# Sample columns of the first FFN's gate and up: from the direct products of chunk 0 (256 of 320 columns stay) into the combined products of chunks 1 and 2 (416 columns each)

## The chip, the core and the metric

The kernel runs on one core of one Trainium2 chip. The metric is the device time of one launch in microseconds (us). Before the change the median of three runs is 1937.2 us (1936.32 to 1937.89).

A core has five engines with a queue each: TensorE (PE, matrix products into PSUM; loads of the stationary operand are shown as PEld), VectorE (DVE), ScalarE (ACT), GpSimd (POOL) and SyncE (SP), which here issues nearly all DMAs. SBUF has 128 partitions; "columns" are elements along the free dimension.

## What is computed

One layer of a decoder trunk, for a prompt of 1024 tokens and 64 sample tokens (8 sequences of 8), model width 1024, FFN width 2816:

```
x = x + 0.5 * post1(SwiGLU_1(pre1(x)))                  # first FFN
z = pre_mix(x) @ w_in + b_in                            # mixer: windowed attention and a gated recurrence
x = x + post_mix(concat(norm(attention), gate(recurrence)) @ w_out)
x = x + 0.5 * post2(SwiGLU_2(pre2(x)))                  # second FFN

def rms_norm(x, g):  return x * rsqrt(mean(x * x) + EPS) * g
def swiglu(x, w_gu, w_down):
    g, u = split(x @ w_gu, 2);  return (silu(g) * u) @ w_down
```

All of it is in float32. Outputs are the new x, the key and value windows and the recurrent states. The change concerns the first FFN above all: its pre-norm, its gate and up products, and its down product for one group of tokens.

## The kernel before

**Tokens.** The 1088 tokens lie in three chunks (`WIDTH = [320, 384, 384]`): chunk 0 has prompt tokens 0 to 255 and all 64 sample tokens, chunks 1 and 2 have 384 prompt tokens each. In the FFN's up part features lie on partitions and tokens along columns, in eight slices of 128 features.

**Precision.** Each float32 operand is split into a rounded part and a rest (`hi` by a ScalarE copy, L240; `lo` by a VectorE subtraction, L241), both in float32r. `mm3` (L258) makes a product of three matmuls, hi x hi, hi x lo, lo x hi, at L260, L261 and L262. So nearly every matmul of the trace has one of these three lines.

**Chunk 0 in the first FFN.** `up0` (L730) makes one tile of 128 gate and 128 up features: 2 x 8 x 3 = 48 matmuls of 320 columns. Weights are loaded and split by `load_w`, three weight tiles (of 24 matmuls) ahead (`loads0`, `Ahead`); the tag "wsp" has eight buffers, a hi and a lo for each of four weight tiles. The norm of chunk 0 isn't applied to its input: its root (`f.root`, one number a column) multiplies the gate and the up bank on their way out (`gated0`, L712: L718, L719, L725, L726). 18 of the 22 tiles are made so, ahead of the combined products (`HEAD1 = 9` pairs); the first three by hand in `pre_first`. The other four are cut into pieces (`piece`, L860) that stand between the combined products and use their weights; they need one more weight split, m = 8.

**Chunks 1 and 2 in an FFN.** Their gate and up products are combined: of the 2 x 2 blocks (two chunks, two halves of the features; gate, up) not eight but seven products are made (Strassen's scheme in Winograd's form). A "unit" is one tile of 128 gate and 128 up features for both chunks: 7 products x 4 slices x 3 = 84 matmuls of 384 columns; there are 22 units. The factors on the token side (`f.SF[1]` to `f.SF[7]`) are sums and differences of the normed chunks, made once by `pre_x` and `sums_s` (L525) in the stream `p1`. Those on the weight side are made for each unit by `factor` (L750; L760 and the splits), into buffers of the tags "wsp" and "wf" (4 buffers). `evict` (L790) takes the banks out and `left` (L821) sums them for the down part, which is again of seven products.

**Streams.** Side work is cut into steps by generators. `stream(name, gen, rate)` registers one, each `tick()` in the dense products makes `rate` steps of it, and `need(name)` makes all that are left. `p1` starts behind the first tile of the loop in the "f1" part and has 60 ticks there; `need("p1")` stands behind the head. In the same way `need("c2")` stands ahead of the second FFN's units.

**Order.** A planner of the framework places each engine's instructions from the program's order and its own estimate of times. An engine works in order; so does SP's queue of DMA issues.

**Down, chunk 0.** `down` (L942) makes 2 x 4 banks of 320 columns, and ScalarE copies each out (L963). Its token operand is read back from the DRAM tensor `acts` in pieces (`ar<-act`), through "wf" buffers.

**Mixer.** `mix_consts` (L147) makes masks at the end of the first FFN. The mixer's blocks of attention (`attn_block`, `finish_attn`) and recurrence run as streams beside the dense products of w_in, the rest of the first FFN's down part and the second FFN's head. Temporaries come from the tag "t2" (8 buffers), small columns from "small" (10).

Of the kernel before, what the change touches and what calls it, by code (L numbers as in the profile page):

```python
# [18 lines left out]
P = 128  # L19
# [6 lines left out]
WIDTH = [320, 384, 384]  # L26
BLK0 = [0, 2, 5]
# [20 lines left out]
def tile_step(ctx: ExitStack, tc: tile.TileContext, A: dict, O: list):  # L48
# [74 lines left out]
    ones = cp.tile([P, P], F32, name="ones")  # L123
    V.memset(ones, 1.0)
    junk = cp.tile([P, 512], BF16, name="junk")
    omean = cp.tile([P, P], F32, name="omean")
    V.memset(omean, 1.0 / D)
    S.activation(junk[:, :P], ones, AF.Silu)
    cols = cp.tile([P, NROWS], F32, name="cols")
    f1pre = cp.tile([P, KC], F32, name="f1pre")  # L130
    halfpost = cp.tile([P, 16], F32, name="halfpost")
    nsinkb = cp.tile([P, 8], F32, name="nsinkb")
    amask = cp.tile([P, 192], F32, name="amask")
    amask1 = cp.tile([P, P], F32, name="amask1")
    smask = cp.tile([P, 136], F32, name="smask")
    ssink = cp.tile([P, 2], F32, name="ssink")
    seqm = cp.tile([P, 4], F32, name="seqm")
    lmask = {h: cp.tile([P, 32], U8, name=f"lm{h}") for h in LEVELS[2:]}
    ident32 = cp.tile([P, 32], F32, name="ident32")
# [3 lines left out]
    def gains():  # L143
        nc.sync.dma_start(cols, A["cols"])
        V.tensor_scalar(halfpost[:, 0:8], cols[:, C_F1POST:C_F1POST + 8], 0.5, None, op0=ALU.mult)
        V.tensor_scalar(halfpost[:, 8:16], cols[:, C_F2POST:C_F2POST + 8], 0.5, None, op0=ALU.mult)

    def mix_consts():
# [4 lines left out]
        band = tmp2("band", (P, 256))  # L153
        V.memset(band, 0.0)
        G.affine_select(band, band, pattern=[[1, 256]], compare_op=ALU.is_ge, fill=NEG,
                        base=0, channel_multiplier=-1)
        G.affine_select(band, band, pattern=[[-1, 256]], compare_op=ALU.is_ge, fill=NEG,
                        base=P, channel_multiplier=1)
        V.tensor_copy(amask[0:64], band[0:64, 0:192])
        V.tensor_copy(amask[64:P], band[64:P, 64:256])  # L160
        V.tensor_copy(amask1, amask[:, 64:192])
        V.memset(amask1[0:64, 0:64], NEG)
# [5 lines left out]

        s5 = tmp[:, 3, 0:32]
        V.tensor_scalar(s5, row[:, 0:32], 31, None, op0=ALU.bitwise_and)  # L170
        V.tensor_tensor(x[:, 0:32], col[:, 0:32], s5, op=ALU.bitwise_xor)
        V.tensor_copy(tf[:, 1, 0:32], s5)
        V.tensor_copy(tf[:, 1, 32:64], col[:, 0:32])
        V.tensor_tensor(tf[:, 0, 0:32], tf[:, 1, 32:64], tf[:, 1, 0:32], op=ALU.is_gt)
        V.tensor_tensor(ident32, tf[:, 1, 32:64], tf[:, 1, 0:32], op=ALU.is_equal)
        for i, h in enumerate(LEVELS[2:]):
            V.tensor_scalar(tmp[:, 3, 32:64], x[:, 0:32], 4 - i, None, op0=ALU.logical_shift_right)
            V.tensor_copy(tf[:, 1, 64:96], tmp[:, 3, 32:64])
            V.scalar_tensor_tensor(lmask[h], tf[:, 1, 64:96], 1.0, tf[:, 0, 0:32],
                                   op0=ALU.is_equal, op1=ALU.mult)  # L180
# [16 lines left out]
        V.tensor_tensor(smask, tf2[:, 2], tf2[:, 3], op=ALU.add)  # L197

        e = cp.tile([P, 3, 4], F32, name="lbe")
# [34 lines left out]
    def small():  # L234
        return pp.tile([P, 4, 8], F32, tag="small", bufs=10, name=uid("sm"))
# [51 lines left out]
    def tmp2(name, shape=(P, 512)):  # L287
        return pp.tile(list(shape), F32, tag="t2", bufs=8, name=uid(name))
# [177 lines left out]
    def factor(SF, m, src):  # L466
        new = (lambda: hslot(1)) if m in (1, 2, 4, 5) else (lambda: big(F32R))
        hi, lo = SF[m] = new(), new()
        S.copy(hi, src)
        yield  # L470
        V.tensor_tensor(lo, src, hi.bitcast(F32), op=ALU.subtract)
        yield

    def pre_x(n, y, gpre, part, SF):
# [5 lines left out]
        yield from bcast_steps(x_part, 384, rb, True)  # L480
# [10 lines left out]
    def pre_s(n, y, gpre, part, SF, dst=None):  # L491
# [15 lines left out]
        for kh in range(2):  # L507
            a = big()
            part[n].append(a)
            for k in range(4):  # L510
# [4 lines left out]
                if k % 2:  # L515
                    V.tensor_scalar(a[:, k], bank[:, :384], g, None, op0=ALU.mult)
                else:
                    S.activation(a[:, k], bank[:, :384], AF.Copy, scale=g)
# [6 lines left out]
    def sums_s(part, SF):  # L525
        (a11, a12), (a21, a22) = part[1], part[2]
        s1, s2 = big(), big()
# [13 lines left out]
    x2T = dr.tile([P, KC, WIDTH[0]], F32, name="x2T")  # L541
    x1N = [dr.tile([384, D], F32, name=f"x1N{n}") for n in range(2)]
    x2N = [dr.tile([384, D], F32, name=f"x2N{n}") for n in range(2)]

    def load_x(n):
        y = [big(), big()]
        for hf in range(2):
            nc.sync.dma_start(y[hf], A["xT"][n - 1][:, 4 * hf * 384:4 * (hf + 1) * 384].rearrange("p (k t) -> p k t", k=4))
# [5 lines left out]
    def load_first(ws):  # L554


        w = WIDTH[0]
        x = [big(F32, (P, 4, w)), big(F32, (P, 4, w))]
        raws = [big(F32, (P, KC, P)) for _ in ws]

        def x_cols(d, n):
            nc.sync.dma_start(x[d // 4][:, d % 4:d % 4 + n], x0_part(d, n))
# [19 lines left out]
    def pre_first(x, gpre, h, raws, wts):  # L582
# [3 lines left out]
        w = WIDTH[0]  # L586
        spare = axbank()
        for _ in range(WARM):
            warm = PE.matmul(spare[:, :P], ones, ones, start=True, stop=True).ins
# [78 lines left out]
        order("V", made[2])  # L668
# [1246 lines left out]
```

## Time and profile before

| | |
|---|---|
| median of three runs | 1937.2 us (1936.32 to 1937.89) |
| span of the profiled execution | 1937.4 us |
| HBM read / written | 290.86 / 83.39 MB |
| mean DMA rate over the span | 193 GB/s |
| first FFN: head and units | 0 to about 494 us |
| down, chunk 0 | about 494 to 571 us |
| mixer and what runs beside it | about 640 to 1330 us |
| second FFN's units and down | from about 1386 us |

The stages are read from TensorE's instructions in order of time. The profile was taken by the hardware's profiler in one execution. Busy time of an engine is the time covered by its instructions. A matmul's record lasts longer than the distance to the next one's start, since they are pipelined, so a busy TensorE says nothing yet of its pace; the distance from start to start does.

### The profile page before, as it was taken

To read this page: it belongs to the slowest core of one execution; us is meant where nothing else is said; L and a number is where in the kernel's file an instruction comes from. 1 tells how busy PE (TensorE), PEld (TensorE's weight loads), DVE (VectorE), ACT (ScalarE), POOL (GpSimd) and SP (SyncE) were. 2 spreads that over 40 slices of the span, in tenths; PEclk is the share of its full clock that TensorE was granted. 3 is DMA by queue.
4 is the path that set the end of the run, shared out by engine and by line. 5 is a ranking of instruction groups with operands and counts; after the bars stand their busy time and mean duration, and the time that the engine had idled before them with its cause. 6 is when DMAs were issued, how large, how long until landed. Compare 5 with 4: busy or idle time off the path is not lost.

```text
span 1937.4 us, 34843 instructions
## 1 busy us (share of the span) xinstructions
PE 1923.1 (99%) x13547; PEld 1806.1 (93%) x13547; DVE 1430.7 (74%) x2469; ACT 946.0 (49%) x1701; POOL 186.1 (10%) x227
## 2 busy tenths in 40 slices
PE   9999999999999999999999999999999999999998
PEld 9999999999998987788999888989999999999886
DVE  6896789877568666787678758756987887656666
ACT  5553444444455434545445545846544444445452
POOL 0300000000004022020221212000000000000102
PEclk9999999999999999999999999999999999999999
DMA  6643676555767556765334344546555555667974
GB/s 248 209 133 115 232 267 247 206 191 184 242 217 242 180 155 215 283 220 163 114 102 153 99 140 142 164 147 209 185 198 192 198 188 189 210 228 241 308 255 141
DMA packets 175750, 375.56 MB, mean 194 GB/s; under 512 B 16144, under 2 KB 67536, under 8 KB 175568
## 3 DMA queue, kind: packets, MB, share of 16 engines
q1 hardware_dynamic: 169680, 362.84, 56.0%
q10 hardware_dynamic: 5904, 10.49, 1.5%
q8 instruction: 106, 1.74, 0.4%
q14 instruction: 60, 0.49, 0.1%
HBM read 290.86 MB, written 83.39 MB: 193 GB/s over the span
## 4 chain that ended last, share of the span: by engine, by line
PE 88%; DMA 6%; DVE 3%; ACT 1%; issue 1%; POOL 1%; SPq 0%; ACTq 0%; DVEq 0%; POOLq 0%
PE mm L260 27%; PE mm L262 26%; PE mm L261 26%; DMA ar<-fa 1%; DMA xt<-in_x_rest_dram 1%; DMA ar<-act 1%; PE lv L1337 1%; PE sc L1237 1%; DMA raw<-in_ffn_w_gu_dram 1%; PE pv L1283 1%; DVE w L241 1%; PE pT L1269 1%; PE c L262 0%; PE c L260 0%; PE c L261 0%
## 5 line engine op out<-in xcount | busy, mean ns | idle before, releaser
L260 PE MATMUL mm<-h,wsph 128*128 128x320 f32 (+1 forms) x1344 | 427.2, 319 | 0.4 <-DVE big L814 0.4
L261 PE MATMUL mm<-h,wsph 128*128 128x320 f32 (+1 forms) x1344 | 425.5, 317 | 0.2 <-DVE h L241 0.2
L262 PE MATMUL mm<-h,wspl 128*128 128x320 f32 (+1 forms) x1344 | 422.6, 316 | 0.0
L241 DVE TENSOR_TENSOR wspl<-raw,wsph 128x1024 fp32r<-128x1024 f32 x208 | 260.8, 1255 | 125.2 <-ACT wsph L240 124.1
L240 ACT CAST wsph<-raw 128x1024 fp32r<-128x1024 f32 x208 | 217.8, 1049 | 254.0 <-PE mm L261 199.3
L260 PEld LDWEIGHTS mm<-h,wsph 128*128 128x128 f32 x1344 | 252.2, 188 | 4.2 <-issue 2.3
L261 PEld LDWEIGHTS mm<-h,wsph 128*128 128x128 f32 x1344 | 252.5, 188 | 3.9 <-issue 2.3
L262 PEld LDWEIGHTS mm<-h,wspl 128*128 128x128 f32 x1344 | 251.9, 188 | 3.4 <-issue 3.1
L240 ACT CAST w<-raw 128x512 fp32r<-128x512 f32 (+1 forms) x208 | 153.8, 745 | 199.9 <-PE mm L261 96.2
L261 PE MATMUL mm<-h,w 128*128 128x384 f32 (+1 forms) x736 | 245.6, 334 | 0.3 <-DVE h L622 0.3
L260 PE MATMUL mm<-h,w 128*128 128x384 f32 (+1 forms) x736 | 245.7, 334 | 0.2 <-ACT h L620 0.2
L262 PE MATMUL mm<-h,w 128*128 128x384 f32 (+1 forms) x736 | 239.6, 333 | 0.5 <-POOL w L613 0.4
L241 DVE TENSOR_TENSOR w<-raw,w 128x512 fp32r<-128x512 f32 (+1 forms) x208 | 178.3, 861 | 72.6 <-ACT w L240 71.7
L261 PE MATMUL mm<-w,h 128*128 128x512 f32 x462 | 180.5, 391 | 0.7 <-DVE w L241 0.7
L260 PE MATMUL mm<-w,h 128*128 128x512 f32 x462 | 180.8, 394 | 0.0
L262 PE MATMUL mm<-w,h 128*128 128x512 f32 x462 | 179.8, 391 | 0.0
L260 PE MATMUL mm<-big,w 128*128 128x384 f32 x528 | 176.7, 335 | 0.3 <-ACT big L806 0.2
L261 PE MATMUL mm<-big,w 128*128 128x384 f32 x528 | 176.5, 334 | 0.0
L262 PE MATMUL mm<-big,w 128*128 128x384 f32 x528 | 176.0, 334 | 0.0
L261 PEld LDWEIGHTS mm<-h,w 128*128 128x128 f32 x736 | 138.1, 188 | 1.1 <-DVE h L622 0.8
L260 PEld LDWEIGHTS mm<-h,w 128*128 128x128 f32 x736 | 138.1, 188 | 0.8 <-ACT h L620 0.5
L262 PEld LDWEIGHTS mm<-h,w 128*128 128x128 f32 x736 | 137.6, 188 | 1.0 <-POOL w L613 0.7
(367 smaller groups left out, 3353.8 us busy)
## 6 DMA issues: line engine op xcount, KB each, us to landing
raw<-in_ffn_w_gu_dram SPq DMA_DIRECT2D x162, 512.0 KB
raw<-in_ffn_w_down_dram SPq DMA_DIRECT2D x74, 512.0 KB
raw<-in_w_in_dram SPq DMA_DIRECT2D x54, 512.0 KB
ar<-fa SPq DMA_DIRECT2D x70, 384.0 KB
big<-in_ffn_w_down_dram SPq DMA_DIRECT2D x88, 256.0 KB
fb<-big SPq DMA_DIRECT2D x44, 512.0 KB
fa<-big SPq DMA_DIRECT2D x22, 768.0 KB
raw<-fb SPq DMA_DIRECT2D x30, 512.0 KB
```

The source lines that it names most:

```text
L240: made['S'] = S.copy(hi, src).ins
L241: (lo_eng or V).tensor_tensor(lo, src, hi.bitcast(F32), op=ALU.subtract)
L260: PE.matmul(out, a[0], b[0], start=first, stop=False, skip_group_check=resume)
L261: PE.matmul(out, a[0], b[1], start=False, stop=False, skip_group_check=resume)
L262: return PE.matmul(out, a[1], b[0], start=False, stop=last, skip_group_check=resume).ins
L1237: PE.matmul(banks[g][rows(hq), i, cs], zq[rows(g), 2 * pr + i, b * P + 64 * hq:b * P + 64 * hq + 64], kx[rows(g), k0 + cs.start:k0 + cs.st ...
L1269: PE.transpose(tb2[hq][:, g, i, slot], pt[g][rows(hq), c:c + P], ident[rows(hq), rows(hq)])
L1283: PE.matmul(ob[par][rows(g), :, hq], vn[rows(par), b + (blk + hq) // 2, rows(g)], pT[hq][rows(par), g, :, PLACE[hq][blk]], start=alone or ...
L1337: PE.matmul(b5[32 * i:32 * i + 32, b, a], K[:, a, cs], Q[:, a, cs], start=True, stop=True)
```

## The change

Each of the chunks 1 and 2 takes 32 sample tokens into the first FFN's gate and up part, as columns 384 to 415 behind its own (`WS = 416`); chunk 0 keeps 256 prompt columns there (`WU`). The host lays the input out so. All 22 tiles of chunk 0 are now made in the head (`HEAD1 = NK`), and pieces, their step kinds and the split m = 8 are gone. `acts` gets prompt columns from `gated0` and sample columns from `evict`. Chunk 0's root is still applied to the gate, but for the up factor only at the down projection, on the 256 prompt columns, from a copy kept in DRAM (`rootd`). The sample columns are normed with their chunk.

The streams p1 and c2 are no longer emptied ahead of the units: a product takes the next steps of the stream until its factor is there (`feed`). p1 starts one tile earlier, chunk 1's input is loaded before the loop, and the split of factor 5 goes to GpSimd.

The wider buffers take room in SBUF. For it "t2" has 7 buffers, "small" 5 and "wf" 3; masks are made when the mixer starts (`amask` in bf16), or kept in DRAM (`smask`, `ownd`), the bias row is loaded for each chunk, and the attention's gain is applied behind the transposes, from the columns of `cols`. `f1pre` and the halved gains lie in `cols` too. In the second FFN's head ScalarE's Silu reads the bank directly.

```diff
+WU, XT = 256, 32
+WS = 384 + XT
...
-        return pp.tile([P, 4, w], F32R, tag=f"h{w}", bufs=8 if w == 384 else 4, name=uid("h"))
+        return pp.tile([P, 4, WS if w == 384 else w], F32R, tag=f"h{w}", bufs=8 if w == 384 else 4, name=uid("h"))
-    def big(dt=F32, shape=(P, 4, 384)):
+    def big(dt=F32, shape=(P, 4, WS)):
...
+    def feed(name):
+        gen = streams[name][0]
+        while True:
+            yield next(gen)
...
     def small():
-        return pp.tile([P, 4, 8], F32, tag="small", bufs=10, name=uid("sm"))
+        return pp.tile([P, 4, 8], F32, tag="small", bufs=5, name=uid("sm"))
-        return pp.tile(list(shape), F32, tag="t2", bufs=8, name=uid(name))
+        return pp.tile(list(shape), dt, tag="t2", bufs=7, name=uid(name))
...
     def factor(SF, m, src):
-        hi, lo = SF[m] = new(), new()
+        hi, lo = new(), new()
         S.copy(hi, src)
         yield
-        V.tensor_tensor(lo, src, hi.bitcast(F32), op=ALU.subtract)
+        (G if m in (5,) else V).tensor_tensor(lo, src, hi.bitcast(F32), op=ALU.subtract)
+        SF[m] = hi, lo
         yield
     def pre_x(n, y, gpre, part, SF):
-        yield from bcast_steps(x_part, 384, rb, True)
+        yield from bcast_steps(x_part, WS, rb, True)
...
         def gated0(j, g, rb):
-            w = WIDTH[0]
+            w = wu
             t = tmp2("sg")
-            if rb is None:
-                S.copy(t[:, :w], g[:, :w])
-            else:
+            if rb is not None:
                 V.tensor_tensor(t[:, :w], g[:, :w], rb, op=ALU.mult)
-            S.activation(t[:, :w], t[:, :w], AF.Silu)
+            S.activation(t[:, :w], g[:, :w] if rb is None else t[:, :w], AF.Silu)
             def rest(u):
-                v = u
-                if rb is not None:
-                    v = tmp2("su")
-                    V.tensor_tensor(v[:, :w], u[:, :w], rb, op=ALU.mult)
-                V.tensor_tensor(t[:, :w], t[:, :w], v[:, :w], op=ALU.mult)
-                return nc.sync.dma_start(acts[:, j], t[:, :w]).ins
+                V.tensor_tensor(t[:, :w], t[:, :w], u[:, :w], op=ALU.mult)
+                return nc.sync.dma_start(acts[:, j, :w], t[:, :w]).ins
...
-                w = f.pool.tile([P, 2, 512], F32R, tag="wf", bufs=4, name=uid("w"))
+                w = f.pool.tile([P, 2, 512], F32R, tag="wf", bufs=3, name=uid("w"))
...
         def product(u, m):
+            while m not in f.SF:
+                next(f.feed)
-            bk = chains[u, c][:, :384]
+            bk = chains[u, c][:, :ws]
...
         def evict(u, m):
             elif m == 3:
-                V.tensor_tensor(e[:, 1], bk, e[:, 1], op=ALU.add)
+                V.tensor_tensor(e[:, 1, :ws], bk, e[:, 1, :ws], op=ALU.add)
                 act(0)
+                if tag == 1:
+                    nc.sync.dma_start(acts[:, j, WU:].rearrange("p (h t) -> p h t", h=2), e[:, 0:3:2, 384:])
...
         def down(last=None):
+                    if tag == 1 and kp == NK - 2:
+                        rt = tmp2("rt")[:, :WU]
+                        nc.sync.dma_start(rt, rootd)
...
-                            S.copy(y[hf][:, i, :w], bank[:, :w])
+                            if tag == 1:
+                                V.tensor_tensor(y[hf][:, i, :WU], bank[:, :WU], rt, op=ALU.mult)
+                                S.copy(y[hf][:, i, WU:w], bank[:, WU:w])
+                            else:
+                                S.copy(y[hf][:, i, :w], bank[:, :w])
...
         def finish_attn(n, o, r, sl):
-            V.scalar_tensor_tensor(o[:r], o[:r], sm[:r, 1, 0:1], aon[:r], op0=ALU.mult, op1=ALU.mult)
+            S.activation(o[:r], o[:r], AF.Copy, scale=sm[:r, 1, 0:1])
...
-            put_mix(n, 0, sl, b4[:, :, :r])
+            hi, lo = MT[n][0][0], MT[n][1][0]
+            for c in range(4):
+                g = cols[:, C_AON + c:C_AON + c + 1]
+                S.activation(hi[:, c, sl], b4[:, c, :r], AF.Copy, scale=g)
+                V.scalar_tensor_tensor(lo[:, c, sl], b4[:, c, :r], g, hi[:, c, sl].bitcast(F32), op0=ALU.mult,
+                                       op1=ALU.subtract)
...
-    HEAD1, HEAD2 = 9, (4, 13, 22)
+    HEAD1, HEAD2 = NK, (4, 13, 22)
...
+        def p1():
+            yield from pre_x(1, xs[1], f1pre, part, f1.SF)
+            yield from pre_x(2, xs[2], f1pre, part, f1.SF)
+        xs.append(load_x(1))
         for j in first[3:]:
+            if j == first[3]:
+                stream("p1", p1(), P1)
             stored = f1.up0(j, w0)
-            if j in XAT:
+            if j == first[3]:
                 with tc.issue_after(stored):
-                    xs.append(load_x(len(xs)))
-            if j == XAT[0]:
-                def p1():
-                    yield from pre_x(1, xs[1], f1pre, part, f1.SF)
-                    yield from pre_x(2, xs[2], f1pre, part, f1.SF)
-                stream("p1", p1(), P1)
-        f1.begin(units(HEAD1))
-        need("p1")
+                    xs.append(load_x(2))
+        f1.begin(UNITS)
+        f1.feed = feed("p1")
...
-        f2.begin(units(NK))
-        need("c2")
+        f2.begin(UNITS)
+        f2.feed = feed("c2")
```

More of the change, by code (lines that the diff above doesn't have):

```diff
@@ L526, in sums_s @@
         (a11, a12), (a21, a22) = part[1], part[2]
-        s1, s2 = big(), big()
+        s1, s2 = [big()[:, :, :a11.shape[2]] for _ in range(2)]
         V.tensor_tensor(s1, a21, a22, op=ALU.add)
@@ L582, in pre_first @@
     def pre_first(x, gpre, h, raws, wts):
[L586 removed]
+        w = WU
         spare = axbank()
         for _ in range(WARM):
[L589 removed]
+            warm = PE.matmul(spare[:, :P], omean, omean, start=True, stop=True).ins
         tiles = [None] * len(raws)
```

256 lines of the change are left out of this document (125 added, 131 removed).

## The prediction, made before the changed kernel was built or run

> **What bounds the kernel now.** I read the page first, then the groups of instructions with shapes kept apart, then TensorE's timeline for the pace of one matmul, and last the windows for places where another engine is close behind.
>
> ```profile
> span 1937.4 us, 34843 instructions
> PE 1923.1 (99%) x13547; PEld 1806.1 (93%) x13547; DVE 1430.7 (74%) x2469; ACT 946.0 (49%) x1701; POOL 186.1 (10%) x227
> PE 88%; DMA 6%; DVE 3%; ACT 1%; issue 1%; POOL 1%; SPq 0%; ACTq 0%; DVEq 0%; POOLq 0%
> ```
> ```profile
> 60.00 0.31 PE L260 MATMUL mm<-h,wsph 128*128 128x320 f32 x1
> 67.04 0.31 PE L260 MATMUL mm<-h,wsph 128*128 128x320 f32 x1
> 380.16 0.33 PE L260 MATMUL mm<-big,w 128*128 128x384 f32 x1
> 384.32 0.33 PE L260 MATMUL mm<-h,w 128*128 128x384 f32 x1
> 622.70 0.39 PE L260 MATMUL mm<-w,h 128*128 128x512 f32 x1
> 624.74 0.39 PE L260 MATMUL mm<-w,h 128*128 128x512 f32 x1
> ```
>
> TensorE is busy 99% of the span, and the chain that ended last is 88% TensorE. What a matmul costs is not its duration (0.31 us), because they overlap, but the distance from start to start. The three pairs of rows are the ends of 48, 24 and 9 intervals (48 is sixteen rounds of L260, L261, L262): 7.04/48 = 146.7 ns at 320 columns, 4.16/24 = 173.3 ns at 384, 2.04/9 = 226.7 ns at 512. The three lie on one line: 13.3 ns plus 0.4167 ns a column. By it 256 columns take 120.0 ns and 416 take 186.7 ns (estimates; neither width runs in this trace).
>
> The profile gives a span and no other time of its own execution. 1937.4 us lies 0.2 above the median of the three runs, so differences worked out from it are taken off 1937.2.
>
> **The columns.** The direct products of chunk 0 are 22 tiles x 2 (gate, up) x 8 slices x 3 = 1056 matmuls: 18 tiles in the head (864) and 4 as pieces between the combined products (192).
>
> ```profile
> L260 PE MATMUL mm<-h,w 128*128 128x384 f32 x704 | 235.4, 334 | 0.0
> ...
> L260 PE MATMUL mm<-big,w 128*128 128x384 f32 x528 | 176.7, 335 | 0.3 <-ACT big L806 0.2
> ```
>
> The two groups of one of three lines give (704 + 528) x 3 / 2 = 1848 combined products for each FFN. All counts stay. The direct products go from 146.7 to 120.0 ns: 1056 x 26.7 ns = 28.2 us less. The combined ones go from 173.3 to 186.7 ns: 1848 x 13.3 ns = 24.6 us more. Net **-3.5 us** (before rounding). The fixed part cancels; what is left is 1056 x 64 - 1848 x 32 = 8448 columns.
>
> The unknown is the pace at 256. The nearest rows on both sides are 320 columns, 146.7 ns, and transposes of 128 columns, each with a weight load of its own.
>
> ```profile
> 828.23 1.47 PE L457 MATMUL tr<-ident,big 128*128 128x128 f32 x12
> ```
> ```profile
> L457 PE MATMUL tr<-ident,big 128*128 128x128 f32 x48 | 7.1, 273 | 0.0
> ```
>
> Twelve of them take 1.47 us, the last 0.27 of it its own duration, so (1.47 - 0.27)/11 = 109 ns. Loads of 128 columns can follow each other at least that fast, so they don't stop a pace of 120.0 ns, which I take. The ends are 109 ns (11.6 us more gained) and 146.7 ns (28.2 us not gained); from 123.3 ns on the change costs matmul time instead of saving it.
>
> **VectorE while chunks 1 and 2 are prepared.** The stream p1 (norm, gains, sums and their splits) runs beside the direct tiles, whose own VectorE work is two weight splits and three (after: two) products with a bank.
>
> ```profile
> 100.00:132.00 32.00, 32.00 (x220) 32.00 (x219) 32.00 (x39) 16.94 (x18) 0.00 (x0) 1.00 0.46 136
> 60.00:100.00 40.00, 40.00 (x273) 39.73 (x272) 34.87 (x46) 22.14 (x30) 8.98 (x6) 1.00 0.58 187
> ```
> ```profile
> L241 DVE TENSOR_TENSOR wspl<-raw,wsph 128x1024 fp32r<-128x1024 f32 x8 | 9.7, 1218 | 0.0
> L483 DVE SCALAR_TENSOR_TENSOR big<-big,f1pre,rb 128x384 f32<-128x384 f32 x8 | 4.4, 608 | 0.0
> L471 DVE TENSOR_TENSOR big<-big,big 128x1536 fp32r<-128x1536 f32 x2 | 3.5, 1750 | 0.0
> L471 DVE TENSOR_TENSOR h<-big,h 128x1536 fp32r<-128x1536 f32 x2 | 3.5, 1750 | 0.0
> L725 DVE TENSOR_TENSOR su<-mm,rb 128x320 f32<-128x320 f32 x5 | 2.4, 485 | 0.0
> L718 DVE TENSOR_TENSOR sg<-mm,rb 128x320 f32<-128x320 f32 x5 | 2.4, 484 | 0.0
> L726 DVE TENSOR_TENSOR sg<-sg,su 128x320 f32<-128x320 f32 x4 | 1.9, 485 | 0.0
> L530 DVE TENSOR_TENSOR big<-big,big 128x1536 f32<-128x1536 f32 x1 | 1.8, 1751 | 0.0
> ```
> ```profile
> L241 DVE TENSOR_TENSOR wspl<-raw,wsph 128x1024 fp32r<-128x1024 f32 x11 | 15.0, 1367 | 2.2 <-ACT wsph L240 2.2
> L726 DVE TENSOR_TENSOR sg<-sg,su 128x320 f32<-128x320 f32 x5 | 4.3, 861 | 0.1
> ...
> L725 DVE TENSOR_TENSOR su<-mm,rb 128x320 f32<-128x320 f32 x6 | 2.9, 481 | 0.0
> L718 DVE TENSOR_TENSOR sg<-mm,rb 128x320 f32<-128x320 f32 x5 | 2.4, 483 | 0.1
> ```
>
> In a row of the windows stand the stretch, its length, then busy time and count of PE, PEld, DVE, ACT and POOL, the clock granted (1.00) and the DMA share and rate. From 100 to 132 us VectorE is busy for all of 32.00 us, and TensorE still runs dense (220 matmuls x 146.7 ns = 32.3 us). It is the one place where another engine is at its limit. The eight groups are those of 100 to 132 us, the four behind them of 60 to 100.
>
> From 100 to 132 there are 220/48 = 4.6 tiles. The groups add up to 35.5 us (four like L530, and one of 0.6 us) in 32.00, because successive instructions overlap: a factor of 0.90. p1 has 19.1 of them, 17.2 us by the factor; the tiles 14.8. After, p1 is 416/384 as wide and one of its splits (1.75 us) goes to GpSimd: 17.2 x 1.083 - 1.7 = 16.9 us. A tile needs 2 x 1.218 us for the splits and two products of 256 columns at 0.41 us (an estimate from 0.484 us at 320, 0.0011 us a column), so 4.6 x 3.26 x 0.90 = 13.5 us. Together that is 30.4 us in 4.6 x 48 x 120.0 ns = 26.5 us of matmuls: **3.9 us too much.** From 60 to 100 us (5.7 tiles) the tiles have 24.6 x 0.90 = 22.1 us of the 34.87, p1 12.8; after, 12.8 x 1.083 + 5.7 x (2 x 1.367 + 0.82) x 0.90 = 32.1 of 32.8 us, so nothing is saved up there.
>
> GpSimd's split has a price too.
>
> ```profile
> 50.85 1.65 DVE L241 TENSOR_TENSOR wspl<-raw,wsph 128x1024 fp32r<-128x1024 f32 x1
> 53.64 2.04 DVE L241 TENSOR_TENSOR wspl<-raw,wsph 128x1024 fp32r<-128x1024 f32 x1
> 56.01 1.64 DVE L241 TENSOR_TENSOR wspl<-raw,wsph 128x1024 fp32r<-128x1024 f32 x1
> 50.25 6.31 POOL L311 TENSOR_TENSOR ss<-ss,sq 128x384 f32<-128x384 f32 x4
> ```
> ```profile
> L1585 POOL TENSOR_TENSOR big<-big,big 128x1024 f32<-128x1024 f32 x4 | 10.0, 2511 | 32.0 <-PE sav L1582 32.0
> ```
>
> Beside 6.31 us of GpSimd additions three VectorE splits took 1.65, 2.04 and 1.64 us instead of 1.218: 1.7 us too much, 0.27 us for each us of GpSimd. A split of 1664 columns is about 2.51 x 1664/1024 = 4.1 us on GpSimd, so it adds 1.1 us: 5.0 us too much in all.
>
> The Trainium skill, "SBUF — State Buffer", section "Who interferes with whom", says that a VectorE instruction with two SBUF inputs and a GpSimd one that reads SBUF shut each other out for the whole instruction. By that rule the 4.1 us would be lost whole, and the wait below 3.0 us longer. The row of 2.04 us shows only a part of the time lost, and the measurement decides.
>
> ```profile
> L240 ACT CAST wsph<-raw 128x1024 fp32r<-128x1024 f32 x208 | 217.8, 1049 | 254.0 <-PE mm L261 199.3 <-DMA raw<-in_ffn_w_down_dram 16.5 <-issue 11.8
> ```
>
> The cover is that weights are split three tiles of 24 matmuls ahead: 3 x 24 x 120.0 ns = 8.6 us, less one cast and one split (1.05 + 1.22), so 6.3 us if it is full when the stretch begins. 5.0 fits in 6.3, but little refills it before. I take **+1.0 us** of waiting TensorE. The ends are 0 and 9.6 us: no cover, and no overlap of instructions, so that full durations count in both stretches (33.8 - 26.5 = 7.3; 20.2 + 13.8 - 32.8 = 1.2; the lock 1.1).
>
> **The other edits.**
>
> ```profile
> 0.00:20.00 20.00, 17.80 (x104) 16.35 (x105) 13.09 (x25) 15.51 (x29) 1.98 (x7) 1.00 0.84 305
> 470.00:500.00 30.00, 29.38 (x181) 28.86 (x180) 20.18 (x59) 17.68 (x27) 0.33 (x2) 1.00 0.58 195
> 715.00:900.00 185.00, 182.39 (x1621) 150.18 (x1620) 141.55 (x314) 87.72 (x198) 36.39 (x39) 1.00 0.68 226
> 1130.00:1330.00 200.00, 199.27 (x2035) 178.61 (x2034) 134.88 (x286) 119.42 (x254) 20.50 (x32) 1.00 0.48 154
> ```
> ```profile
> 481.29 3.67 DMA ar<-act
> ```
>
> Four more tiles bring eight weight loads of 512 KB into the head: 1 MB for each 5.76 us, 182 GB/s, where the first 20 us moved 305. Chunk 1's input goes ahead of the tiles on SP's queue, before the fourth raw weight: 1.7 MB at 305 GB/s is 5.6 us, covered by the weights already loaded. In the units a VectorE operation grows by 32 x 0.0011 us and the unit by 84 x 13.3 ns = 1.1 us, so there is more cover than before. Forming products lazily instead of emptying p1 and c2 first, and masks that no longer fall at the end of the first FFN, can remove the 0.62 us of idle TensorE from 470 to 500 us; I take **-0.3**.
>
> At the down projection the eviction is a product on VectorE beside a small copy, under six matmuls of the next bank: nothing. There "wf" has three buffers for four, and the last unit's sample columns are stored just before they are loaded. If a load comes late, the next weights wait behind it on SP, and it costs one landing like the 3.67 us row. Two tiles of 24 x 146.7 ns = 7.0 us hide it; I take 0, end +3.7.
>
> In the mixer the norm's gain moves behind the transposes, six instructions more for each of nine blocks; ScalarE has 178 of 385 us idle in the two windows of it. Fewer "t2" (7 for 8) and "small" (5 for 10) buffers can make blocks wait for one another. TensorE idles 2.6 + 0.7 us there now; I take **+0.3**, from -2 to twice that idle time again, +4.
>
> Sum: -3.5 + 1.0 - 0.3 + 0.3 = -2.5, so **1934.7 us**.
>
> **The rivals.** (1) *All of it is kept*: the splits stay ahead and idle places go, -3.5 - 0.6 - 1.3 (of the mixer's -2) = **1931.8 us**. For it: the cover of 6.3 us. (2) *VectorE becomes the bound in p1*, the slower end: TensorE waits for weight splits. The full 9.6 us give 1937.2 - 3.5 + 9.6 = **1943.3 us**; from 7.4 us of waiting on, the result is slower than before by 0.2%. For it speaks 32.00 of 32.00; against it, that TensorE stayed dense beside that. (3) *The weight load sets the pace at 256*: at 146.7 ns nothing is saved there, -3.5 + 28.2, **1961.9 us**; against it stands the 109 ns. The Trainium skill, "TensorE: Matmul & The Clock Gate", section "LDWEIGHTS (loading the stationary operand)", gives a load its columns divided by 1.2 in ns, an estimate from that page of 106.7 ns for 128; 256 columns stream just as long, so a load would have no room left, yet the 109 ns agrees with the page and lies under 120. (4) *Fewer buffers in the mixer*, at their end: -3.5 + 1.0 - 0.3 + 4 = **1938.4 us**, and 1942.1 with the late load at the down projection. (5) *The change doesn't bring what it says*: columns are saved, and waits take all of it, **1937.2 us**.
>
> **How the numbers follow.** A measurement of this kernel can tell about 0.2%, 3.9 us. Forecast 0.40, its own range 1933.4 to 1937; (1) 0.36; (2) 0.11; (3) 0.03; (4) 0.06, half of it with the late load; (5) 0.04. Faster by over 0.2%: 0.36. Within: 0.40 + 0.03 + 0.04 = 0.47. Slower: 0.11 + 0.03 + 0.03 = 0.17. The range takes in (1), (4), (5) and the nearer part of (2): 1929.5 to 1942.5.
>
> **What would show it.** Right: 120.0 ns from start to start at 256 columns and 186.7 at 416; VectorE full for some 26 us of the head, with TensorE's weight loads waiting there about 1 us for splits; a smaller VectorE share in the units. Wrong: a pace above 123 ns; several us of weight loads waiting for VectorE in the head; a longer stretch between the two FFNs.

## The result and the profile after

| | before | after |
|---|---|---|
| median | 1937.55 us (1936.32 to 1939.19, 4 runs) | 1970.56 us (1967.74 to 1972.76, 4 runs) |
| ratio | | 1.0166, 95% interval 1.0152 to 1.0180 |
| span of the profiled execution | 1937.4 us | 1966.0 us |

The change makes the kernel 33 us slower; forecast was 1934.7 us with an upper end of 1942.5. The profiled execution of after is the fastest of its four, so the traces have to account for the 28.6 us between the two spans. Of the page of after, the span, the busy time of the engines, and the chain that ended last:

```profile
span 1966.0 us, 35068 instructions
...
PE 1942.7 (99%) x13547; PEld 1810.9 (92%) x13547; DVE 1441.1 (73%) x2474; ACT 960.3 (49%) x1719; POOL 203.4 (10%) x230
...
PE 85%; DVE 5%; DMA 4%; ACT 2%; issue 2%; POOL 1%; SPq 0%; ACTq 0%; DVEq 0%; POOLq 0%
```

The same 13547 matmuls, TensorE still "busy" for 99%, and yet 19.6 us more of it (1942.7 against 1923.1). The share says nothing of it, and it is a first hint that the matmuls themselves have become slower. The starts of the first matmul of each stage in TensorE's timeline give the lengths of the stages (us):

| stage | before | after | difference |
|---|---|---|---|
| first FFN: head and units | 485.8 | 496.2 | +10.4 |
| first FFN: down, chunk 0 | 73.9 | 73.2 | -0.7 |
| first down pair to the second FFN's units (mixer) | 808.7 | 819.6 | +10.9 |
| second FFN: units | 325.2 | 327.9 | +2.7 |
| second FFN: down, chunk 0, and the down pairs | 230.6 | 235.8 | +5.2 |

The second FFN's units and pairs have the same instructions and shapes as before. TensorE's timeline of after tells what happened there. The rows are pairs: the first and the last of 48 intervals at 256 columns, 84 at 416, 84 at 384 (second FFN), 30 at 512 (second FFN's pairs).

```profile
121.81 0.28 PE L245 MATMUL mm<-h,wsph 128*128 128x256 f32 x1
127.58 0.28 PE L245 MATMUL mm<-h,wsph 128*128 128x256 f32 x1
379.75 0.35 PE L244 MATMUL mm<-big,w 128*128 128x416 f32 x1
395.62 0.35 PE L244 MATMUL mm<-big,w 128*128 128x416 f32 x1
1499.75 0.34 PE L246 MATMUL mm<-h,w 128*128 128x384 f32 x1
1514.49 0.34 PE L246 MATMUL mm<-h,w 128*128 128x384 f32 x1
1879.67 0.40 PE L245 MATMUL mm<-w,h 128*128 128x512 f32 x1
1886.67 0.40 PE L245 MATMUL mm<-w,h 128*128 128x512 f32 x1
```

5.77/48 = 120.2 ns at 256 columns, as forecast. 15.87/84 = 188.9 ns at 416, not 186.7. 14.74/84 = 175.5 ns at 384, where it was 173.3, and 7.00/30 = 233.3 ns at 512, where it was 226.7. TensorE waits for no other engine in these stretches: the matmuls themselves are a little slower.

The head is another matter. The windows of after (columns as in the prediction) and its waits from 60 to 120 us:

```profile
60.00:80.00 20.00, 16.47 (x132) 15.74 (x131) 18.78 (x21) 11.75 (x19) 12.26 (x6) 1.00 0.62 196
100.00:120.00 20.00, 16.85 (x124) 16.30 (x123) 20.00 (x18) 10.80 (x11) 5.05 (x1) 0.91 0.35 118
```
```profile
PE rb L279 <- POOL ss L295: 2.6, 1, 2.6
PE mm L244 <- DVE sg L705: 2.6, 2, 1.4
...
PEld mm L244 <- ACT big L453: 1.5, 1, 1.5
...
PE mm L244 <- DVE sg L709: 0.9, 1, 0.9
...
PE mm L246 <- DVE wspl L225: 0.6, 1, 0.6
```

132 and 124 matmuls need about 15.8 and 14.9 us at 120.0 ns, so 4.2 and 5.1 us are lost, **9.3 us** in all. The listed waits of TensorE's matmuls are 6.7 us of it. One, 2.6 us, is its own matmul of the root (`rb`, L279), which waits for GpSimd's additions. The others end on VectorE: 3.5 us on the products that read a gate or an up bank (L705, L709) and so set it free, and only 0.6 us on a weight split (L225). One weight load (PEld) waits 1.5 us for ScalarE. In the second stretch the granted clock also falls to 0.91; its listed waits are 3.2 us, and 5.1 are lost.

### The profile page after: what moved, and what is told of

The parts are those of the page before. It is cut to its first block, busy times and chain, and to the rows that moved or that the text cites. A ratio compares the mean times of both kernels' runs of the same rounds, so it can differ in the third digit from the quotient of the medians.

```text
span 1966.0 us, 35068 instructions
## 1 busy us (share of the span) xinstructions
PE 1942.7 (99%) x13547; PEld 1810.9 (92%) x13547; DVE 1441.1 (73%) x2474; ACT 960.3 (49%) x1719; POOL 203.4 (10%) x230
## 4 chain that ended last, share of the span: by engine, by line
PE 85%; DVE 5%; DMA 4%; ACT 2%; issue 2%; POOL 1%; SPq 0%; ACTq 0%; DVEq 0%; POOLq 0%
PE mm L244 27%; PE mm L245 27%; PE mm L246 27%; DMA raw<-in_ffn_w_gu_dram 1%; DVE wspl L225 1%; PE lv L1337 1%; POOL ss L295 1%; PE pT L1269 1%; DMA xt<-x1T 0%; PE sc L1237 0%; PE pv L1283 0%; ACT wsph L224 0%; DMA ar<-act 0%; DMA x1N<-big 0%; DMA gb<-in_norm_ffn_post_dram 0%
## 5 line engine op out<-in xcount | busy, mean ns | idle before, releaser
L244 PE MATMUL mm<-h,wsph 128*128 128x320 f32 (+2 forms) x1408 | 439.8, 314 | 5.4 <-DVE sg L705 2.6
L245 PE MATMUL mm<-h,wsph 128*128 128x320 f32 (+2 forms) x1408 | 438.8, 312 | 0.1
L246 PE MATMUL mm<-h,wspl 128*128 128x320 f32 (+2 forms) x1408 | 436.8, 311 | 1.1 <-DVE wspl L225 1.1
L225 DVE TENSOR_TENSOR wspl<-raw,wsph 128x1024 fp32r<-128x1024 f32 x216 | 268.4, 1244 | 121.0 <-ACT wsph L224 116.2
L224 ACT CAST wsph<-raw 128x1024 fp32r<-128x1024 f32 x216 | 226.0, 1048 | 254.2 <-PE mm L245 179.7
L244 PEld LDWEIGHTS mm<-h,wsph 128*128 128x128 f32 x1408 | 265.8, 189 | 10.9 <-issue 4.3
L245 PEld LDWEIGHTS mm<-h,wsph 128*128 128x128 f32 x1408 | 266.5, 189 | 4.5 <-issue 3.5
L246 PEld LDWEIGHTS mm<-h,wspl 128*128 128x128 f32 x1408 | 266.2, 189 | 3.9 <-issue 1.8
L244 PE MATMUL mm<-h,w 128*128 128x384 f32 (+2 forms) x736 | 252.2, 343 | 0.9 <-ACT h L607 0.9
L246 PE MATMUL mm<-h,w 128*128 128x384 f32 (+2 forms) x736 | 251.5, 342 | 0.7 <-POOL w L600 0.4
L245 PE MATMUL mm<-h,w 128*128 128x384 f32 (+2 forms) x736 | 250.8, 341 | 0.4 <-DVE h L609 0.3
L225 DVE TENSOR_TENSOR w<-raw,w 128x512 fp32r<-128x512 f32 (+1 forms) x204 | 173.7, 854 | 64.7 <-ACT w L224 63.0
L244 PE MATMUL mm<-big,w 128*128 128x416 f32 (+1 forms) x528 | 182.3, 345 | 0.2 <-ACT big L791 0.2
L246 PE MATMUL mm<-big,w 128*128 128x416 f32 (+1 forms) x528 | 181.9, 345 | 0.0
L245 PE MATMUL mm<-big,w 128*128 128x416 f32 (+1 forms) x528 | 181.3, 343 | 0.0
L224 ACT CAST w<-t 128x512 fp32r<-128x512 f32 x176 | 107.8, 619 | 86.7 <-PE mm L246 83.5
L245 PEld LDWEIGHTS mm<-h,w 128*128 128x128 f32 x736 | 138.4, 188 | 1.9 <-DVE h L609 0.8
L244 PEld LDWEIGHTS mm<-h,w 128*128 128x128 f32 x736 | 138.4, 188 | 1.9 <-ACT h L607 1.1
```

Of the source, the lines that this page charges most:

```text
L224: made['S'] = S.copy(hi, src).ins
L225: (lo_eng or V).tensor_tensor(lo, src, hi.bitcast(F32), op=ALU.subtract)
L244: PE.matmul(out, a[0], b[0], start=first, stop=False, skip_group_check=resume)
L245: PE.matmul(out, a[0], b[1], start=False, stop=False, skip_group_check=resume)
L246: return PE.matmul(out, a[1], b[0], start=False, stop=last, skip_group_check=resume).ins
```

## The experiments

The first theory on the slow matmuls was the rows: the tiles of tags "h384" and "big" have rows of 416 elements (1664 bytes) instead of 384 (1536). Its rival: the whole pool starts at another byte than before.

**e1_rows1536**

```diff
-    def big(dt=F32, shape=(P, 4, WS)):
+    def big(dt=F32, shape=(P, 4, 384)):
-                outs[u] = big()
+                outs[u] = big(F32, (P, 4, ws))
...
-        new = (lambda: hslot(1)[:, :, :src.shape[2]]) if m in (1, 2, 4, 5) else (lambda: big(F32R)[:, :, :src.shape[2]])
+        new = (lambda: hslot(1, ww)) if m in (1, 2, 4, 5) else (lambda: big(F32R, (P, 4, ww)))
```

> The changed kernel, with the tiles that hold no sample columns cut back to rows of 384 elements (1536 bytes); only the first FFN's gate/up factors and outputs keep rows of 416 (1664 bytes). Every slot starts where it did. Theory 'rows' (a matmul slows down when an operand lies in a tile with rows of 1664 bytes): the second FFN's products of 384 columns return from 175.5 to 173.3 ns (1848 x 2.2 = 4 us), the down pairs of 512 columns from 232.7 to 226.7 ns (1386 x 6.0 = 8 us), the mixer's products 1 to 4 us, so 13 to 16 us off the changed kernel's 1970.6: 1954 to 1958 us; the products of 416 columns stay at 188.8 ns. Theory 'start' (what counts is that the whole pool starts at another byte, 0 instead of 32 modulo 64): no pace changes, 1968 to 1973 us.

**e2_before_shift288** and **e4_after_shift32** put an unused tile ahead of the pool (`pad = cp.tile([P, 72], F32)` in before, `[P, 8]` in after).

> The kernel before, with an unused tile of 288 bytes ahead of the pool, so that all its tiles start at the same phase (128 modulo 512, 0 modulo 64) as those of the changed kernel. Theory 'start': 384 columns go from 173.3 to 175.5 ns (3696 x 2.2 = 8 us), 512 columns from 226.7 to 232.7 (1386 x 6.0 = 8 us), so 1953 to 1958 us. Theory 'rows': no pace changes, 1937 to 1938 us.

> The changed kernel, with an unused tile of 32 bytes ahead of the pool, so that its tiles start at 32 modulo 64 bytes as those of the kernel before. Theory 'start': the paces return to 173.3 ns at 384 columns, 226.7 at 512 and 186.7 at 416, 16 to 19 us off 1970.6: 1951 to 1955 us. Theory 'rows': nothing changes, 1968 to 1973 us.

Measured: e1 1961.1 us (ratio to before 1.0122, 1.0105 to 1.0139), e2 1937.47 us (1.0001, 0.9992 to 1.0011), e4 1971.7 us (1.0176, 1.0160 to 1.0191). The pool's start does nothing, the rows do: the second FFN's pairs take 157.5 us again, as before. But e1 stays short of its forecast, and TensorE's timeline of e1, 84 intervals in the second FFN's units, shows where:

```profile
1499.79 0.34 PE L246 MATMUL mm<-big,w 128*128 128x384 f32 x1
1514.48 0.34 PE L246 MATMUL mm<-big,w 128*128 128x384 f32 x1
```

174.9 ns, with all rows back at 1536 bytes. Sorted by the buffer of the weights, the starts give 173.4 ns with "wsp" and 176.1 ns with "wf". By the sizes of the tiles in the program, "wf" stands in its own pool behind the "small" buffers, and with five of these, of 128 bytes each, instead of ten it begins 128 bytes off modulo 256; before, all of "big", "h384", "wsp" and "wf" began at 96 modulo 256. Rows of 1664 bytes (6.5 x 256) do the same to every second row. That made the next theory: what counts is the distance modulo 256 bytes between the moving rows and the stationary ones.

**e5_wf_aligned** (on e1; the same in pool f2), **e6_before_wsp128** and **e9_before_wsp64** (on before; e9 with 64 and 192 bytes for 128 and 128):

```diff
         f1.pool = tp
+        V.memset(tp.tile([P, 32], F32, name="pad1"), 0.0)
```
```diff
         h[0] = new_h(0)
+        V.memset(pp.tile([P, 8], F32, tag="t2", bufs=8, name="pad0"), 0.0)
+        V.memset(pp.tile([P, 32], F32, tag="pada", bufs=1, name="pada"), 0.0)
...
+    V.memset(pp.tile([P, 32], F32, tag="padb", bufs=1, name="padb"), 0.0)
```

> e1_rows1536 with 128 unused bytes ahead of the 'wf' buffers, so that they too start at 128 modulo 256 bytes, as the tokens and 'wsp' do. Theory 'phase' (a matmul slows down where its moving rows and the stationary rows next to it in time start 128 bytes apart modulo 256): the second FFN's products with 'wf' weights go from 176.1 to 173.4 ns, as those with 'wsp' weights have it already; 1056 x 2.7 = 2.9 us off 1961.1, so 1958 us, and the second FFN's units take 1 us more than before the change or less. Theory 'rows' (only rows of 1664 bytes are slow): nothing changes, 1961 us, and the 176.1 ns have another cause.

> The kernel before, with 128 unused bytes ahead of the 'wsp' buffers and 128 behind 'raw', so that 'wsp' alone is 128 bytes modulo 256 away from all other tiles; no row gets longer. Theory 'phase': the down pairs go from 226.7 to 232.7 ns (1386 x 6.0 = 8.3 us), the combined products with 'wsp' weights from 173.3 to 176 (1584 x 2.7 = 4.3 us), the mixer's products 1 to 3 us; 1950 to 1953 us. Theory 'rows': 1937 us, no pace changes.

> The kernel before, with 64 unused bytes ahead of the 'wsp' buffers and 192 behind 'raw': 'wsp' alone is 64 bytes modulo 256 away from all other tiles, where e6_before_wsp128 had 128 and 15 us more. Theory 'any phase' (equal starts modulo 256 are needed): slower by half of that or more, 1944 to 1953 us. Theory 'half' (only 128 bytes apart is slow): 1936 to 1938 us.

Measured: e5 1957.3 us (1.0106, 1.0088 to 1.0124), e6 1952.15 us (1.0076, 1.0061 to 1.0091), e9 1945.81 us (1.0043, 1.0028 to 1.0058). The intervals of e1 and e5 overlap, but the second FFN's units take 324.0 us in e5 and 326.5 in e1. And 128 unused bytes in the kernel before cost 15 us. TensorE's timelines, of e5 (84 intervals at 384, 24 at 512), e6 (15 at 512) and e9 (21 at 512):

```profile
1499.77 0.33 PE L245 MATMUL mm<-big,w 128*128 128x384 f32 x1
1514.33 0.33 PE L245 MATMUL mm<-big,w 128*128 128x384 f32 x1
1879.79 0.39 PE L244 MATMUL mm<-w,h 128*128 128x512 f32 x1
1885.23 0.62 PE L244 MATMUL mm<-w,h 128*128 128x512 f32 x2
```
```profile
1881.77 0.39 PE L260 MATMUL mm<-w,h 128*128 128x512 f32 x1
1885.26 0.40 PE L260 MATMUL mm<-w,h 128*128 128x512 f32 x1
```
```profile
1881.30 0.39 PE L260 MATMUL mm<-w,h 128*128 128x512 f32 x1
1886.10 0.39 PE L260 MATMUL mm<-w,h 128*128 128x512 f32 x1
```

e5 is back at 14.56/84 = 173.3 and 5.44/24 = 226.7 ns. e6 has 3.49/15 = 232.7 ns, the pace of after, in the kernel before; e9 has 4.80/21 = 228.6. In the second FFN's units the weights that were moved pay and the others don't (ns, means over most of its 792 matmuls with "wsp" and 1056 with "wf"):

| weights | before | e6: "wsp" 128 bytes off | e9: "wsp" 64 off | e5 |
|---|---|---|---|---|
| "wsp" | 173.3 | 176.0 | 176.5 | 173.3 |
| "wf" | 173.4 | 173.8 | 173.6 | 173.3 |

Theory "phase" holds at 384 and 512 columns, in both directions. The start itself doesn't count: all of the operands begin at 96 modulo 256 in before and at 128 in e5, and both have 173.3 ns. At 320 columns the direct products of e6 keep 146.7 ns.

**e14_rows1792** (on e5) asks whether the same explains 416 columns:

```diff
-        new = (lambda: hslot(1, ww)) if m in (1, 2, 4, 5) else (lambda: big(F32R, (P, 4, ww)))
+        new = (lambda: hslot(1, 448 if ww == WS else ww)[:, :, :ww]) if m in (1, 2, 4, 5) else (lambda: big(F32R, (P, 4, ww)))
-        return pp.tile(list(shape), dt, tag="big", bufs=12, name=uid("big"))
+        return pp.tile(list(shape), dt, tag="big", bufs=11, name=uid("big"))
```

> e5_wf_aligned with rows of 448 elements (1792 bytes, 7 x 256) for the token factors 1, 2, 4 and 5 (moving operand 'h'), while 3, 6 and 7 ('big') keep rows of 1664 bytes, and 11 'big' buffers instead of 12. Theory 'phase': the 416-column products with 'h' go from 188.8 ns to 186.7 or 187.0, those with 'big' stay at 189.0; 1056 x 2.0 = 2.1 us less than e5's 1957.3, so about 1955 us, if 11 buffers cost nothing. Rival 'the line is not straight' (416 columns cost more than the line of three widths says): both stay at 188.8 to 189.0 ns, 1957 us.

Measured: 1962.91 us (1.0136, 1.0119 to 1.0153); 188.2 ns with "h", 189.1 with "big". Mostly a miss: aligned rows win 0.6 of the 2.1 ns. What makes 416 columns 1.5 ns dearer than the line of three widths stays open. It is the one of the five widths 256, 320, 384, 416 and 512 that is no multiple of 64 columns (256 bytes), and no run tried another such width. Its mixer is 4.7 us longer than that of e5, beside one "big" buffer less.

**The head: e3_p1_065, e7_no_gpsimd_split, e11_no_gpsimd** (e3 on after, e7 on e1, e11 on e7):

```diff
-P1 = 1.0
+P1 = 0.65
```
```diff
-        (G if m in (5,) else V).tensor_tensor(lo, src, hi.bitcast(F32), op=ALU.subtract)
+        V.tensor_tensor(lo, src, hi.bitcast(F32), op=ALU.subtract)
```
```diff
-            sum_squares(G if add else V, ss[:, :w], sq[:, :w], d)
+            sum_squares(V, ss[:, :w], sq[:, :w], d)
```

> The changed kernel, with the stream p1 at 0.65 steps a tick instead of 1.0, so that its 49 steps use all 76 ticks of the head. Theory 'VectorE bound in p1' (TensorE waits some 9.7 us from 60 to 120 us because VectorE has more work there than matmuls run beside it): the wait falls under 2 us, 1961 to 1964 us. Rival 'transfers' (the weights arrive late because chunk inputs and four more tiles are loaded there): the wait stays near 9 us, 1968 to 1973 us.

> e1_rows1536 with the split of factor 5 back on VectorE. Theory 'GpSimd holds VectorE up' (the split takes 6.8 us on GpSimd, and a VectorE operation on 4 columns took 3.76 us behind it): TensorE's waits from 100 to 116 us (3.6 us, and a slower clock behind them) shrink to under 1.5; 1956 to 1959 us. Rival 'VectorE has too much work there anyway': one more split of 1.9 us on VectorE, so the waits stay or grow, 1961 to 1963 us.

> e7_no_gpsimd_split with the sums of squares of p1 on VectorE too, so that GpSimd does nothing in p1. Theory 'GpSimd holds VectorE up': TensorE's matmul of the root no longer waits 2.8 us at 71 us for GpSimd's additions (6 of them took 12.7 us there), VectorE's splits beside it take 1.22 us again and not 1.5 to 2.1; 1953 to 1956 us. Rival 'VectorE has too much work': 14 additions of about 0.6 us more on VectorE, 8 us, so the waits move and stay, 1957 to 1961 us.

Measured: e3 1968.28 us (1.0157, 1.0142 to 1.0172). That is a miss for its theory and the figure of its rival, late transfers: the head shrinks by 8.5 us and the units grow by 6.6. The waits have mostly moved to a later stretch, where VectorE is busy throughout, as a window of e3 shows:

```profile
120.00:140.00 20.00, 15.64 (x121) 14.53 (x119) 20.00 (x17) 12.26 (x14) 7.56 (x1) 1.00 0.37 123
```

From 120 to 160 us TensorE's matmuls wait 5.1 us there, 4.5 of them for VectorE (L705, L709, L225) and 0.6 for a weight copy on ScalarE. Copies of weights wait 14.0 us for DMAs in that stretch, so late transfers may have a small part. e7 1957.75 us (1.0100, 1.0085 to 1.0115), 3.4 us under e1 (the intervals just overlap; head and units are 4.7 us shorter in the traces, 493.3 us; but they take 497.1 to 500.9 us in e1, e5 and e8, which are alike there, so the size is uncertain). e11 1960.51 us (1.0119, 1.0104 to 1.0134), not faster than e7: the rival's figure. Both have a part of the truth. First GpSimd's, in the timelines of VectorE and GpSimd in after, and of VectorE in e7:

```profile
98.37 1.89 DVE L517 TENSOR_TENSOR big<-big,big 128x1664 f32<-128x1664 f32 x1
100.17 1.22 DVE L225 TENSOR_TENSOR wspl<-raw,wsph 128x1024 fp32r<-128x1024 f32 x1
101.31 3.76 DVE L186 TENSOR_TENSOR lbe<-cols,lbe 128x4 f32<-128x4 f32 x1
98.20 6.84 POOL L455 TENSOR_TENSOR h<-big,h 128x1664 fp32r<-128x1664 f32 x1 [23.75 <-ACT h L453]
```
```profile
101.22 0.15 DVE L186 TENSOR_TENSOR lbe<-cols,lbe 128x4 f32<-128x4 f32 x1
```

A subtraction of four columns takes 0.15 us alone and 3.76 us beside GpSimd's split; both end at about 105.05 us. The trace is read so: GpSimd's 6.84 us begin with a wait of 3 us for VectorE, and then VectorE stands still for all of its 3.6 us of work. The Trainium skill, "SBUF — State Buffer", section "Who interferes with whom", says just this (a VectorE instruction with two SBUF inputs and a GpSimd one that reads SBUF block each other in full), and here the trace agrees. In e3 GpSimd's record is longer, 7.56 us, and the same subtraction still takes 3.78 us; e1, e4, e5, e8 and e14, which keep GpSimd's split, have 3.75 to 3.76.

The rest is VectorE's amount of work: e11 takes GpSimd out altogether, and its waits only move, as its windows show (TensorE 16.13 and 16.85 of 20 us, the first with a granted clock of 0.83):

```profile
80.00:100.00 20.00, 16.13 (x110) 15.63 (x109) 17.07 (x29) 7.83 (x11) 0.00 (x0) 0.83 0.46 149
100.00:120.00 20.00, 16.85 (x137) 16.27 (x135) 20.00 (x19) 12.48 (x12) 0.00 (x0) 1.00 0.36 119
```

**The mixer: e8_finish_before** (on e1; it leaves out the attention norm's gain):

```diff
-            S.activation(o[:r], o[:r], AF.Copy, scale=sm[:r, 1, 0:1])
+            V.scalar_tensor_tensor(o[:r], o[:r], sm[:r, 1, 0:1], o[:r], op0=ALU.mult, op1=ALU.mult)
...
-                S.activation(hi[:, c, sl], b4[:, c, :r], AF.Copy, scale=g)
-                V.scalar_tensor_tensor(lo[:, c, sl], b4[:, c, :r], g, hi[:, c, sl].bitcast(F32), op0=ALU.mult,
-                                       op1=ALU.subtract)
+            put_mix(n, 0, sl, b4[:, :, :r])
```

> e1_rows1536 with the end of the attention block in the instructions of the kernel before (one VectorE product ahead of the transposes, one copy and one subtraction behind them); the attention norm's gain is replaced by the value itself. Theory 'ScalarE's extra steps': of the 7.4 us by which the stretch from the first down pair to the second FFN's units is longer than before, 3 or more go; 1955 to 1958 us. Rival 'fewer buffers' (7 't2' and 5 'small'): the stretch stays within 1 us, 1960 to 1962 us.

Measured: 1955.47 us (1.0094, 1.0079 to 1.0109), 5.6 us under e1 (the intervals just overlap); the stretch is 2.2 us longer than before instead of 7.4. The same stretch also differs by 3 us between e1 and e7 (4.4), which are alike in it, so 2 to 5 us are the end of the norm's. How it costs, from after, one line's instructions with what they waited for:

```profile
L1206 ACT ACTIVATE h<-oT,cols x36: 293/367/372, 794.7 to 1310.2; 128x128 fp32r<-128x128 f32 x32, 128x64 fp32r<-128x64 f32 x4
...
  DVE h L1207: 18.7, 19
```

The copies of ScalarE (L1206) and the subtractions of VectorE (L1207) take turns, four times a block: ScalarE stands 18.7 us in 19 waits for VectorE, and all behind it in its queue stands too.

**All together.** e10_all joins e11, e5 and a cheaper end of the norm's (the first lines below; its scaling by the root also goes to VectorE); e12_all_p1_08 is e10 with P1 = 0.8; e13_spread is e12 with twice the room for the sums' steps (the second lines); e15_spread_rows1792 is e13 with e14's rows; e16_joined_065 is e5 with factor 5's split on VectorE, e10's end of the norm's and P1 = 0.65, and keeps GpSimd's sums of squares.

```diff
+            g = cols[:, C_AON:C_AON + 4].unsqueeze(2).to_broadcast([P, 4, r])
+            V.tensor_tensor(b4[:, :, :r], b4[:, :, :r], g, op=ALU.mult)
+            put_mix(n, 0, sl, b4[:, :, :r])
```
```diff
-            yield from sums_s(part, SF)
+            for _ in sums_s(part, SF):
+                yield
+                yield
```

> e11_no_gpsimd with 'wf' aligned (as in e5_wf_aligned), and the attention norm's end in one VectorE scaling, one VectorE product with the gains behind the transposes, one copy and one subtraction. If the causes are separate, their parts add up from 1961.1: 'wf' -3.8, GpSimd's split -3.4, its sums -2 to -4, the norm's end -2 to -5: 1945 to 1950 us. If the waits in the head or in the mixer only pass from one engine to the next, 1950 to 1955 us.

> e10_all with p1 at 0.8 steps a tick. If VectorE is over its limit only where p1 runs at full rate, 1 to 4 us less than e10_all, as the same work is spread over 61 ticks for 49; if what is late then is late for the units instead, as in e3_p1_065, within 1 us of e10_all.

> e12_all_p1_08 with each of the 11 steps that form the sums and their factors given two ticks' turns instead of one, so that p1's 60 steps take 75 of the head's 76 ticks and the heavy ones (a VectorE operation of 1.9 us each) are twice as far apart. Theory 'burst' (VectorE is over its limit only while the heavy steps follow each other): of the 8.3 us of waits from 120 to 180 us 4 or more go, 1943 to 1946 us. Rival 'amount' (VectorE's work of the head and the first units doesn't fit beside the matmuls): the waits move into the first units, 1948 to 1951 us.

> e13_spread with the rows of e14_rows1792. If both parts hold and add up, 2 us less than e13_spread: 1941 to 1944 us, still slower than the kernel before; if neither does, 1948 to 1951 us.

> e5_wf_aligned with factor 5's split on VectorE, the attention norm's end as in e10_all, and p1 at 0.65 steps a tick; GpSimd keeps the sums of squares. If p1 at 0.65 gained little in e3_p1_065 because GpSimd's split fell late there, 1943 to 1947 us; if VectorE's work is too much wherever it falls, 1948 to 1951 us. Below 1937 us, the time of the kernel before, would need all waits in the head and the mixer to be gone, which neither theory says.

| | median, us | ratio to before (95%) |
|---|---|---|
| e10_all | 1953.72 | 1.0088 (1.0073 to 1.0103) |
| e12_all_p1_08 | 1949.29 | 1.0072 (1.0055 to 1.0089) |
| e13_spread | 1950.94 | 1.0070 (1.0055 to 1.0085) |
| e15_spread_rows1792 | 1958.54 | 1.0110 (1.0095 to 1.0125) |
| e16_joined_065 | 1945.62 | 1.0039 (1.0025 to 1.0053) |

e10 lands in its second case (1950 to 1955 us): the parts don't add up, for the waits pass from one engine to the next, and its head and units take 498.0 us, near e11's 499.3. e12 is 4.4 us under e10, a little beyond the 1 to 4 of its first case, and the intervals overlap. e13 gives the rival's figure, yet doesn't decide between burst and amount, for the heavy steps still ran together, as VectorE's timeline of e13 shows (five operations of 1.9 us from 117 to 129 us; the line with x2 holds two):

```profile
117.14 1.89 DVE L522 TENSOR_TENSOR big<-big,big 128x1664 f32<-128x1664 f32 x1
118.94 1.89 DVE L456 TENSOR_TENSOR h<-big,h 128x1664 fp32r<-128x1664 f32 x1
...
121.88 3.69 DVE L456 TENSOR_TENSOR big<-big,big 128x1664 fp32r<-128x1664 f32 x2
...
127.28 1.89 DVE L456 TENSOR_TENSOR big<-big,big 128x1664 fp32r<-128x1664 f32 x1
```

The rate of a stream sets when a step is issued in the program; the planner sets where it stands on VectorE. e15 misses: with 11 "big" buffers its mixer is 8.8 us longer than e13's, more than its rows could win. e16 is the best: in it the mixer's stretch is as long as before (808.6 us), the second FFN 0.9 us shorter, and head and units 4.3 us longer; its windows show what is left of the waits:

```profile
100.00:120.00 20.00, 20.00 (x169) 20.00 (x168) 18.84 (x32) 9.24 (x12) 0.00 (x0) 1.00 0.52 168
120.00:140.00 20.00, 16.97 (x132) 16.22 (x132) 20.00 (x18) 12.39 (x14) 0.00 (x0) 0.97 0.39 126
```

25 us of the 33 are won back, and the kernel before is still faster. No version here beats it.

## Why the prediction was wrong

The traces' difference is +28.6 us where the sum had -2.5. Of the 31.1 us between them, 3.9 are the columns, 8.3 VectorE in p1, 7.9 the second FFN and 10.6 the mixer; 0.4 are left.

**The columns.** A step that failed is that of the widths: "The combined ones go from 173.3 to 186.7 ns", with nothing added for any other matmul. The pace at 256 columns is the forecast's 120.0 ns (rival 3 falls), and 28.2 us are saved. But 416 columns take 188.8 ns: 1848 x 15.5 = 28.6 us more. The net is +0.4 instead of -3.5 us: the change has no gain to lose.

**What wasn't in the sum at all.** This is the step that failed most. The forecast read a pace as a matter of columns alone. Wider rows and fewer "small" buffers, which it listed as room in SBUF, moved the operands against each other and slowed matmuls that the change doesn't touch. e1 and e5 together take 13 us off the medians by bytes alone, and e6 puts 15 us onto the kernel before. This is the largest part of the miss: 8 us in the second FFN and, as far as a stretch shows it that varies by 3 us, some 6 in the mixer's (10.9 longer in after, 4.6 in e5).

**VectorE in p1.** Taken +1.0, ends 0 and 9.6; measured 9.3. That VectorE becomes the bound there is what rival 2 says, and it did. But the step on the wait failed: the forecast let TensorE wait for weight splits, and covered that by 6.3 us of weights split ahead. Only 0.6 of the 6.7 us of listed waits end on a split. 3.5 end on the products that set a bank free, which weights split ahead can't cover, and 2.6 on GpSimd's additions, for which the root's matmul waits in TensorE's queue ahead of the products. The forecast costed neither of these waits, nor the lower clock behind them, so it is in part luck that the total comes near the 9.6 us of its slower end. GpSimd's split was mis-sized too: it was priced at 1.1 us from a row in which VectorE lost only part of the time, and here VectorE lost 3.6 us (why that row lost less wasn't tried). The rule of the Trainium skill, weighed there and put aside (4.1 us), was close.

**Mixer.** Taken +0.3 with an end of +4; the stretch is 10.9 longer, of which some 6 are bytes (e1, e5) and 2 to 5 the end of the norm's. The failed step is "ScalarE has 178 of 385 us idle": idle time hides nothing where two engines take turns. That fewer "t2" and "small" buffers cost anything was not tried by itself, nor were the other edits of the mixer: masks that come from DRAM, and the sample attention's output fetched in 8 DMAs instead of 16.

**Right.** The down projection (0 taken, 0.7 us shorter). The -0.3 for p1's end is too small to see.

## What to carry to other kernels

Before a tile gets wider rows, or a pool fewer buffers, see where all operands of the matmuls start modulo 256 bytes afterwards; unequal starts cost 1 to 3% of every matmul at 384 and 512 columns here, and no wait shows it. So compare the distance from start to start in stages that a change doesn't touch. And a pause of GpSimd and VectorE for each other is read from a tiny operation that takes microseconds, not from a mean.

## What the runs showed of the hardware

The pace of a matmul depends on the start of the moving row against that of the stationary one: 226.7, 228.6 and 232.7 ns at 512 columns for 0, 64 and 128 bytes apart modulo 256; 173.3, 176.5 and 176.0 ns at 384; no difference at 320 (146.7 for 128 bytes). Whether it is the load of the next weights that collides with the moving reads was not shown. The Trainium skill, "SBUF — State Buffer", section "Who interferes with whom", gives TensorE two independent read ports, for the moving operand and the weight load; by it the two shouldn't meet, and e6 shows that their addresses matter all the same. The line of the forecast, 13.3 ns plus 0.4167 ns a column, held at 256 columns (120.2 ns measured) and not at 416 (188.2 ns with aligned rows, 186.7 by the line). Pauses of TensorE were followed by a lower granted clock more than once (0.91 from 100 to 120 us in after, 0.83 from 80 to 100 us in e11), so a wait can cost more than its length. Not every pause was: from 60 to 80 us in after 4.2 us are lost, and the clock stays at 1.00.
